# A seventh block of gate columns by seven products, q and k normalized by token tile, and the filling of the forgetting heads laid out anew

## The chip, the cores and the metric

One core of a Trainium2 chip runs the whole layer in one launch. The metric is the device time in microseconds (us). The engines named below are TensorE (PE, whose weight loads the profile lists apart as PEld), VectorE (DVE), ScalarE (ACT), GpSimd (POOL) and SyncE (SP), whose queue issues nearly all transfers.

## The reference

The layer works on x with 1024 tokens of 1024 features in float32. Half a SwiGLU network is added, then two attentions that read the same normalized tokens h, then another half network, and a gated input embedding. What the change touches is the middle:

```python
h = rms_norm(x, mix_norm)
fq, fk, fv, f_logit, sq, sk, sv, g_fox, g_sb = split_columns(h @ w_in)
fq = rms_norm(fq.reshape(b, s, 8, 64), q_norm)      # each token, each head of 64
fk = rms_norm(fk.reshape(b, s, 8, 64), k_norm)
y_fox = forgetting_attention(fq, fk, fv, log_f)     # 8 heads, softmax
y_sb = stick_breaking_attention(sq, sk, sv)         # 8 heads
merged = sigmoid(g_fox) * (y_fox @ w_branch_fox) + sigmoid(g_sb) * (y_sb @ w_branch_sb)
x = x + merged @ w_out
```

The gates g_fox and g_sb are 2048 columns of h @ w_in. The kernel counts them as sixteen gate tiles of 128 columns: 0 to 7 belong to g_fox, 8 to 15 to g_sb. They are needed only when the branches are merged, long after the heads.

## The kernel before

A float32 product is made of three passes over operands split into a high and a low part (fp32r): high by high, high by low, low by high. A product of 128 columns of w_in with 512 tokens over 1024 features takes 3 x 8 = 24 matmuls of 128x512; a gate tile has two halves of 512 tokens, so 48.

The big products are done with a scheme of seven instead of eight block products, called "seven products" here: `make_up` takes a block of 256 columns (two gate tiles) and both halves of tokens and needs seven products of 12 matmuls each (line 556), 84 instead of 96. It costs sums of weight blocks on POOL (`sums`, `last_sum`), splits on ACT and DVE, and some additions when results leave PSUM. `NG` (line 1186) is the number of blocks of 256 gate columns that go this way. Before, it is 6: gate tiles 0 to 11, from 660 to 778 us of the execution. The first block is made in the plain way (line 506), while the block products of the tokens are still being prepared; the others by seven products. The list `hl` names the SBUF slots that hold the split weights of each product, and its last names are those of the last block. `raws["v"]` and `raws["qk"]` are the weights of the next stage, loaded and split in the last products of the gates.

Then come `attention()` and its sixteen heads, eight forgetting ones (numbers 0 to 7 in the order of work) and eight of stick-breaking. A head has four steps c = 0 to 3 of 256 query tokens. `scores` makes the logits (lines 1054, 1055), and for a forgetting head subtracts and reduces on DVE (1059), takes exp on ACT (1065), a reciprocal on DVE (1066) and a product on POOL (1067). `apply`, two steps later, turns the weights with TensorE transposes (1113), splits them on ACT (1115) and DVE (1121), and multiplies with v (1139). Between these pieces of a head the program calls `take()`, which puts other TensorE work there, the filling. `fill[h]` lists the units of head h, and `take()` deals them out in shares per step. The order of TensorE's instructions is the order of these calls. That of the other engines is made by a scheduler at build time; each engine then works in order.

The filling consists of these units:

- `fox_qk_units` (line 852): the q and k columns of a pair of forgetting heads, eight units of 24 matmuls of 128x256 (line 799), one for each tile of 128 tokens. After each unit ACT squares the result (863) and copies it to N (864), and DVE sums the squares per head (865). After every fourth unit come a tensor_scalar on DVE (868), a power of -0.5 on POOL on 128x16 (869), and a product on POOL over all four token tiles, 128x1024 (871).
- `fox_stack_units` (`f[i]`, for head i + 1): four transposes (897) of the normalized q and k of 512 tokens, followed by ACT 884, DVE 885 and four transfers (887) that lay out the operands of `scores`. After each the unit yields a pause of 1.5, which counts as cost with no work.
- `v_units`: the v columns of four heads, eight units of 24 matmuls of 128x256.
- `g_units`: one gate tile, two units of 24 matmuls of 128x512 (line 807), with its own weight load and split (ACT 129, POOL 139). Tiles 12 and 13 lie in forgetting heads and are stored without sigmoid (`raw=True`); the sigmoid is then taken in `load_gate` where the branches are merged. Tiles 14 and 15 lie in stick-breaking heads.
- `sst`: operands of a stick-breaking head, two units of 24 matmuls of 128x512 (line 807 too).

PSUM banks for the filling (tag pf) and for the transposes (tag pt) are two each; a matmul that needs a bank waits until the reader of the work before last has finished.

Of the kernel before, what the change touches and what calls it, by code (L numbers as in the profile page):

```python
# [14 lines left out]
ALU = mybir.AluOpType  # L15
# [21 lines left out]
def tile_hybrid_decoder_layer(  # L37
# [811 lines left out]
    def fox_qk_units(pair, cell, tags=NAT, sq_tag="PT", new_bank=fill_bank):  # L849
        add_load(cell, lambda: mix_nat([(FQ + pair * P, FQ + pair * P + P), (FK + pair * P, FK + pair * P + P)], tags))  # L850

        def unit(t):
# [13 lines left out]
            if q == 3:  # L866
                ss = cell["ss"][half][:].rearrange("p a b -> p (a b)")
                nc.vector.tensor_scalar(ss, ss, 1.0 / HD, EPS, ALU.mult, ALU.add)
                nc.gpsimd.tensor_tensor(ss, ss, mhalf[:], ALU.pow)
                nv = N[:].rearrange("p a h s d -> p (a h s) d")  # L870
                nc.gpsimd.tensor_mul(nv, nv, ss.unsqueeze(2).broadcast_to([P, 16, HD]))
# [47 lines left out]
    def g_units(m, new_bank=fill_bank, raw=False):  # L919
        cell = {}  # L920
        if raw:
            raw_gates.append(m)

        add_load(cell, lambda: wload([kp(win)[:, :, GFOX + m * P:GFOX + m * P + P]], KD, P))

        def unit(half):
            ps = new_bank()
            yield from feat_steps(ps, half, weights(cell))
            g = slot("PT", [P, 512])
            order("act", nc.scalar.copy(g[:], ps[:]) if raw else nc.scalar.activation(g[:], ps[:], AF.Sigmoid))  # L930
            nc.sync.dma_start(gd[m, :, half * 512:half * 512 + 512], g[:])
        return [(24 * 0.216, unit(0)), (24 * 0.216, unit(1))]
# [253 lines left out]
    NG = 6  # L1186

    def mix_start():
# [18 lines left out]
        hl += [cycle[k % 6] for k in range(12, 7 * NG - 6)] + ["WL", "WH", "WH", "Q"]  # L1207
# [56 lines left out]
    def attention():  # L1264
# [8 lines left out]
        def sst(h):  # L1273
            return sb_stack_units(h - 8, stacks[h])
# [16 lines left out]
        def any_bank():  # L1291
# [11 lines left out]
        uq2, g12 = fox_qk_units(fox_pairs[2], qk[2]), g_units(12, raw=True)  # L1303
        uq3, vy = fox_qk_units(fox_pairs[3], qk[3]), v_units(SV, 0, vs0)
        g13, s8, s9 = g_units(13, raw=True), sst(8), sst(9)
# [5 lines left out]
        fill = [mix(f[0], qk1[:7]),  # L1311
                qk1[7:] + vx[:1] + f[1][:1] + vx[1:4] + f[1][1:],
                mix(f[2], vx[4:] + uq2[:3]),
                uq2[3:] + g12[:1] + f[3][:1] + g12[1:] + f[3][1:],
                mix(f[4], uq3[:6]),
                uq3[6:] + vy[:1] + f[5][:1] + vy[1:4] + f[5][1:],
                mix(f[6], vy[4:] + g13[:1]),
                g13[1:] + s8,
# [362 lines left out]
```

## Time and profile before

| what | value |
|---|---|
| median of 3 runs | 2263.2 us (2263.04 to 2263.4) |
| the profiled execution's own time | 2264.1 us |
| its span, first to last instruction | 2262.4 us |
| PE busy | 2235.7 us, 99% of the span |
| DVE, ACT, POOL busy | 1486.8, 989.3, 801.2 us |
| granted TensorE clock | 0.999 |
| forgetting heads, from the first score of head 0 to the first of head 8 | 851.3 to 1113.4 us |

In rows of the profile, "L807 PE MATMUL ps<-H,WH 128*128 128x512 f32 x384 | 115.1, 406 | 0.0" means: line 807 of the program, engine and operation, what is written from what, the shape, how many; then busy us and the mean ns of one; then idle us of the engine before them and what ended it. In a row of a window, each engine's busy us stand with the number of its instructions. A matmul's mean contains its way through a pipelined array, so matmuls follow each other faster than the mean says.

### The profile page before, as it was taken

The numbers are of one execution on the slowest core, as the hardware profiler recorded it, in microseconds if no ns is written. First come the engines' busy times: TensorE is split into PE (matmuls) and PEld (weight loads), VectorE is DVE, ScalarE is ACT, GpSimd is POOL, SyncE is SP. The second block draws the span as 40 slices with busy tenths as digits, with TensorE's granted clock in tenths as the row PEclk, the third lists the DMA queues.
The fourth block names the chain that finished last, engine by engine and source line by source line (L and its number), as shares of the span: only waits on it lengthen the run. The fifth ranks groups of instructions, "written<-read, shape, count | busy, mean of one in ns | idle before, by whom it ended". The sixth has DMA issues, their size and how long they took to land. (4 is left out here: it accounts for less than half of the span.)

```text
span 2262.4 us, 30810 instructions
## 1 busy us (share of the span) xinstructions
PE 2235.7 (99%) x11402; PEld 1900.8 (84%) x11402; DVE 1486.8 (66%) x2303; ACT 989.3 (44%) x1788; POOL 801.2 (35%) x803
## 2 busy tenths in 40 slices
PE   8999999999999999999999999999999999999999
PEld 6888888888888899999898888888888888888888
DVE  8845555688888325666678875889655555778753
ACT  6333333333364445555566663345333333433431
POOL 2444444300011336565567664410544444200121
PEclk9999999999999999999999999999999999999999
DMA  4232323484233333233323366821423232756132
GB/s 140 102 117 85 125 84 125 145 311 172 84 131 113 127 109 110 85 113 85 85 66 91 106 196 232 283 106 55 140 89 121 84 126 84 268 191 217 59 102 85
DMA packets 188936, 291.23 MB, mean 129 GB/s; under 512 B 28393, under 2 KB 104553, under 8 KB 188786
## 3 DMA queue, kind: packets, MB, share of 16 engines
q1 hardware_dynamic: 188784, 289.26, 38.5%
q8 instruction: 90, 1.47, 0.3%
q14 instruction: 60, 0.49, 0.1%
q10 hardware_dynamic: 2, 0.00, 0.0%
HBM read 193.50 MB, written 78.94 MB: 120 GB/s over the span
## 5 line engine op out<-in xcount | busy, mean ns | idle before, releaser
L454 PE MATMUL ps<-H,H 128*128 128x512 f32 x2184 | 497.7, 389 | 1.2 <-DVE X L462 1.2
L454 PEld LDWEIGHTS ps<-H,H 128*128 128x128 f32 x2184 | 409.4, 188 | 86.6 <-issue 2.0
L556 PE MATMUL ps<-H,WL 128*128 128x512 f32 x1116 | 264.9, 389 | 0.8 <-ACT WL L105 0.8
L556 PEld LDWEIGHTS ps<-H,WL 128*128 128x128 f32 x1116 | 209.4, 188 | 44.6 <-ACT WL L105 1.2
L556 PE MATMUL ps<-H,Q 128*128 128x512 f32 x612 | 146.0, 389 | 0.0
L462 DVE SCALAR_TENSOR_TENSOR X<-ps,X 128x512 f32<-128x512 f32 x168 | 109.1, 687 | 50.9 <-PE ps L454 50.9
L556 PEld LDWEIGHTS ps<-H,Q 128*128 128x128 f32 x612 | 114.9, 188 | 23.8
L556 PE MATMUL ps<-X,WL 128*128 128x512 f32 x552 | 132.6, 389 | 0.0
L139 POOL TENSOR_TENSOR WL<-RAW,WH 128x512 fp32r<-128x512 f32 (+1 forms) x84 | 98.5, 1194 | 69.1 <-ACT WH L129 43.2
L556 PEld LDWEIGHTS ps<-X,WL 128*128 128x128 f32 x552 | 103.6, 188 | 21.5
L1121 DVE TENSOR_TENSOR PT<-ps,PT 128x512 fp32r<-128x512 f32 (+1 forms) x160 | 100.0, 627 | 30.9 <-ACT PT L1115 29.7
L799 PE MATMUL ps<-WH,H 128*128 128x256 f32 x768 | 116.1, 288 | 0.8 <-ACT RN L864 0.8
L807 PE MATMUL ps<-H,WH 128*128 128x512 f32 x384 | 115.1, 406 | 0.0
L219 POOL TENSOR_SCALAR ss<-ss 128x1 f32<-128x1 f32 x28 | 9.0, 323 | 296.1 <-ACT WL L215 231.9
L1139 PE MATMUL ps<-PT,X 128*128 128x256 f32 (+1 forms) x640 | 102.7, 286 | 6.9 <-DVE PT L1121 5.8
L556 PE MATMUL ps<-H,PT 128*128 128x512 f32 x456 | 108.9, 389 | 0.0
L1115 ACT CAST PT<-ps 128x512 fp32r<-128x512 f32 (+1 forms) x160 | 87.1, 548 | 42.2 <-PE ps L1113 40.7
L1139 PEld LDWEIGHTS ps<-PT,X 128*128 128x128 f32 x640 | 90.3, 190 | 17.6 <-DVE PT L1121 10.8
L799 PEld LDWEIGHTS ps<-WH,H 128*128 128x128 f32 x768 | 101.4, 190 | 2.7 <-ACT RN L864 1.2
L556 PEld LDWEIGHTS ps<-H,PT 128*128 128x128 f32 x456 | 85.5, 188 | 17.8
L355 POOL TENSOR_TENSOR PT<-GF,RN 128x512 f32<-128x512 f32 x20 | 33.6, 1682 | 184.9 <-DVE GF L710 184.9
L1067 POOL TENSOR_TENSOR T<-T,l 128x128 f32<-128x128 f32 (+3 forms) x64 | 73.2, 1148 | 72.1 <-DVE l L1066 70.0
(436 smaller groups left out, 4889.0 us busy)
## 6 DMA issues: line engine op xcount, KB each, us to landing
hidden<-PT SPq DMA_DIRECT2D x40, 512.0 KB, 3.0
WH<-in_ffn_w_gate_dram SPq DMA_DIRECT2D x38, 512.0 KB, 5.5
Q<-hidden SPq DMA_DIRECT2D x24, 512.0 KB, 5.5
hidden<-RN SPq DMA_DIRECT2D x22, 512.0 KB, 2.6
KH<-in_ffn_w_up_dram SPq DMA_DIRECT2D x20, 512.0 KB, 6.2
KL<-in_ffn_w_up_dram SPq DMA_DIRECT2D x20, 512.0 KB, 6.8
T<-in_ffn_w_down_dram SPq DMA_DIRECT2D x20, 512.0 KB, 7.5
X<-in_x_dram SPq DMA_DIRECT2D x16, 512.0 KB, 10.2
```

Of the source, the lines that this page charges most:

```text
L139: ins = eng_lo.tensor_sub(lo[part], raw[part], f(hi[part]))
L219: nc.gpsimd.tensor_scalar(ss[:], ss[:], EPS, None, ALU.add)
L355: eng.tensor_add(s12[:, 0, :], g1[:, 1, :], g2[:, 1, :])
L454: pe(nc.tensor.matmul(groups[g][t][:], act[:, a, k, t * P:(t + 1) * P], wt[:, b, k, :], start=(fresh and n == 0), stop=(i in (6, 1, 4) and ...
L462: nc.vector.scalar_tensor_tensor(xs, groups[g][t][:], scale, xs, ALU.mult, ALU.add)
L556: pe(nc.tensor.matmul(ps[:], hl[:, a, k, :], rhs(m, b, k), start=(first and i == 0), stop=(final and i == 11), skip_group_check=True))
L799: pe(nc.tensor.matmul(ps[:, :n], hT[t // 4](a, k)[:, (t % 4) * P:(t % 4 + 1) * P], w[k // 4][b][:, k % 4, :n], start=(i == 0), stop=(i == ...
L807: pe(nc.tensor.matmul(ps[:], w[a][:, k, :], hT[half](b, k), start=(i == 0), stop=(i == 23)))
L1067: nc.gpsimd.tensor_mul(T[:, :n], T[:, :n], l[:].broadcast_to([P, n]))
L1115: high = nc.scalar.copy(pt[:, 0, :width], ps[:, :width])
L1121: ins = nc.vector.tensor_sub(pt[:, 1, :width], ps[:, :width], f(pt[:, 0, :width]))
L1139: pe(nc.tensor.matmul(o, lh, r, start=(kpair == c and i == 0), stop=(kpair == 0 and i == 3)))
```

## The change

There are three edits.

1. `NG` is 7: gate tiles 12 and 13 become a seventh block of `make_up`, ahead of the heads, and leave the filling of forgetting heads 3, 6 and 7. With them go their weight loads and splits, and their sigmoids are taken at once. The slots named for the last two products of the last block are KH and KL instead of WH twice.
2. In `fox_qk_units` the tensor_scalar, the power and the product follow every token tile, on 128x4, 128x4 and 128x256, instead of every fourth on 128x16, 128x16 and 128x1024.
3. The lists `fill[0]` to `fill[7]` are written anew. Without the gate tiles, the q, k and v units are dealt so that heads 0 to 3 have 6, 6, 6, 6 units and heads 4 to 7 have 5, 5, 5 and 1, the last with `s8` besides. The second half of the operands of head 4 (`f[3][1:]`) is now made in head 4 itself, after the first half of head 5's (`f[4][:1]`) and one q and k unit.

```diff
-            if q == 3:
-                ss = cell["ss"][half][:].rearrange("p a b -> p (a b)")
-                nc.vector.tensor_scalar(ss, ss, 1.0 / HD, EPS, ALU.mult, ALU.add)
-                nc.gpsimd.tensor_tensor(ss, ss, mhalf[:], ALU.pow)
-                nv = N[:].rearrange("p a h s d -> p (a h s) d")
-                nc.gpsimd.tensor_mul(nv, nv, ss.unsqueeze(2).broadcast_to([P, 16, HD]))
+            ss = cell["ss"][half][:, q, :]
+            nc.vector.tensor_scalar(ss, ss, 1.0 / HD, EPS, ALU.mult, ALU.add)
+            nc.gpsimd.tensor_tensor(ss, ss, mhalf[:, 0:4], ALU.pow)
+            nv = N[:, q].rearrange("p h s d -> p (h s) d")
+            nc.gpsimd.tensor_mul(nv, nv, ss.unsqueeze(2).broadcast_to([P, 4, HD]))
...
-    NG = 6
+    NG = 7
...
-        hl += [cycle[k % 6] for k in range(12, 7 * NG - 6)] + ["WL", "WH", "WH", "Q"]
+        hl += [cycle[k % 6] for k in range(12, 7 * NG - 6)] + ["WL", "KH", "KL", "Q"]
...
-        uq2, g12 = fox_qk_units(fox_pairs[2], qk[2]), g_units(12, raw=True)
-        uq3, vy = fox_qk_units(fox_pairs[3], qk[3]), v_units(SV, 0, vs0)
-        g13, s8, s9 = g_units(13, raw=True), sst(8), sst(9)
+        uq2, uq3 = (fox_qk_units(fox_pairs[i], qk[i]) for i in (2, 3))
+        vy, s8, s9 = v_units(SV, 0, vs0), sst(8), sst(9)
...
-        fill = [mix(f[0], qk1[:7]),
-                qk1[7:] + vx[:1] + f[1][:1] + vx[1:4] + f[1][1:],
-                mix(f[2], vx[4:] + uq2[:3]),
-                uq2[3:] + g12[:1] + f[3][:1] + g12[1:] + f[3][1:],
-                mix(f[4], uq3[:6]),
-                uq3[6:] + vy[:1] + f[5][:1] + vy[1:4] + f[5][1:],
-                mix(f[6], vy[4:] + g13[:1]),
-                g13[1:] + s8,
+        fill = [mix(f[0], qk1[:6]),
+                qk1[6:] + vx[:1] + f[1][:1] + vx[1:3] + f[1][1:] + vx[3:4],
+                mix(f[2], vx[4:] + uq2[:2]),
+                uq2[2:6] + f[3][:1] + uq2[6:],
+                f[4][:1] + uq3[:1] + f[3][1:] + uq3[1:3] + f[4][1:] + uq3[3:5],
+                uq3[5:] + vy[:1] + f[5][:1] + vy[1:2] + f[5][1:],
+                mix(f[6], vy[2:7]),
+                vy[7:] + s8,
```

## The prediction

> **What bounds the kernel now.** I read the page first: the engines' busy shares, then the granted clock, to see whether TensorE has anything to give.
>
> ```profile
> span 2262.4 us, 30810 instructions
> PE 2235.7 (99%) x11402; PEld 1900.8 (84%) x11402; DVE 1486.8 (66%) x2303; ACT 989.3 (44%) x1788; POOL 801.2 (35%) x803
> PEclk9999999999999999999999999999999999999999
> ```
>
> TensorE is busy for all but 26.7 us, at full clock. So a change is worth the matmuls it removes, less the idle time that it makes. Next I read the busy time by windows: first the gates, the stretch after them, and the merging of the branches; then the eight forgetting heads, one row each; then stick-breaking heads 8 to 14.
>
> ```profile
> 680.00:778.00 98.00, 98.00 (x433) 80.87 (x432) 58.61 (x96) 46.04 (x84) 17.36 (x13) 1.00 0.35 119
> 778.90:851.30 72.40, 72.40 (x519) 67.64 (x518) 19.20 (x60) 28.56 (x55) 28.41 (x23) 1.00 0.40 124
> 1400.00:1440.00 40.00, 40.00 (x178) 33.15 (x177) 25.44 (x31) 8.49 (x12) 28.82 (x24) 1.00 0.74 253
> 851.30:881.00 29.70, 28.59 (x223) 27.28 (x222) 15.19 (x60) 15.14 (x37) 18.08 (x16) 1.00 0.43 127
> 881.00:911.30 30.30, 29.11 (x230) 28.01 (x229) 19.36 (x65) 17.15 (x39) 20.32 (x21) 1.00 0.24 62
> 911.30:946.20 34.90, 34.30 (x277) 33.59 (x277) 22.85 (x73) 20.98 (x48) 19.34 (x22) 1.00 0.46 129
> 946.20:985.90 39.70, 39.52 (x278) 36.71 (x277) 21.42 (x69) 21.83 (x49) 26.42 (x25) 1.00 0.21 61
> 985.90:1018.30 32.40, 31.21 (x253) 30.63 (x253) 22.17 (x71) 18.57 (x45) 17.64 (x18) 1.00 0.42 123
> 1018.30:1051.00 32.70, 31.75 (x254) 30.80 (x253) 20.38 (x69) 19.61 (x44) 24.74 (x26) 1.00 0.28 65
> 1051.00:1083.60 32.60, 31.45 (x229) 29.45 (x230) 21.72 (x70) 18.62 (x40) 17.58 (x21) 1.00 0.41 114
> 1083.60:1113.40 29.80, 29.80 (x175) 25.82 (x174) 17.53 (x61) 16.43 (x35) 13.87 (x17) 1.00 0.22 54
> 1113.40:1334.40 221.00, 216.11 (x1326) 190.62 (x1326) 174.13 (x292) 141.66 (x314) 140.20 (x214) 1.00 0.41 111
> ```
>
> The columns are the window, its length, then busy us (instructions) of PE, PEld, DVE, ACT and POOL, the granted clock, and the DMA share with GB/s. The gates leave TensorE no idle time. The heads leave, as length less PE busy, 1.11, 1.19, 0.60, 0.18, 1.19, 0.95, 1.15 and 0.00 us: 6.37 in 262.1. Last the waits in that stretch, to see what makes them.
>
> ```profile
> PE ps L1113 <- DVE PT L1121: 3.0, 4, 1.2
> PE ps L1139 <- DVE PT L1121: 1.1, 4, 0.3
> PE ps L799 <- ACT RN L864: 0.8, 1, 0.8
> PE ps L1139 <- ACT PT L1115: 0.6, 2, 0.5
> ```
>
> In total, times, and the longest: the idle time is mostly TensorE waiting for DVE's low part (1121), which frees a transpose bank or completes an operand.
>
> **The change part by part.** *The matmuls.* In the gates 433 matmuls of 128x512 take 98.00 us, 226.3 ns each. The seventh block adds 7 x 12 = 84 of them, 19.0 us, in a stage without idle time. Two gate tiles less in the heads are 2 x 48 = 96 of the same shape, 21.7 us at the same rate. Balance -2.7 us. In the heads such a matmul also reads longer:
>
> ```profile
> L807 PE MATMUL ps<-H,WH 128*128 128x512 f32 x96 | 27.8, 404 | 0.0
> L807 PE MATMUL ps<-H,WL 128*128 128x512 f32 x48 | 13.2, 397 | 0.0
> L556 PE MATMUL ps<-H,WL 128*128 128x512 f32 x108 | 25.6, 389 | 0.0
> ```
>
> The mean of the first two is 401.7 ns against 389 in the gates, 12.7 more; 96 times that is 1.2 us. If it belonged wholly to these matmuls the balance would be -3.9. But the surplus comes from breaks between filling and head, which are as many as before and now fall on q, k and v units. I take a third, 0.4: -3.1 us.
>
> *What goes along with the gates.* A block in the gates needs POOL, ACT and DVE beside 19 us of TensorE; they have 81, 52 and 39 us free in that 98 us window, so nothing. The first matmul after the gates needs weights that are split in their last products, in slots freed a few products later than before (the low part's last slot by the seventh product of the last block, which has three products, 8.1 us, behind it). POOL does such a low part in halves:
>
> ```profile
> L139 POOL TENSOR_TENSOR WL<-PT,T x4: 1314/1318/1324, 768.4 to 772.3; 128x528 fp32r<-128x528 f32 x4
> ```
>
> Two halves are 2.6 us and fit. If that cover were gone, TensorE would wait those 2.6 us once; the window from 778.90 shows none now. On SP's queue two loads of equal bytes move there and four stores become two, at a DMA share of 0.35. The two late sigmoids leave a stage where ACT is busy 8.49 of 40 us: no gain.
>
> *Normalizing by token tile.* These are the operations in the heads (columns: busy us, mean ns, idle before), and a power and a product of nearly the new size:
>
> ```profile
> L868 DVE TENSOR_SCALAR qkss<-qkss 128x16 f32<-128x16 f32 x6 | 3.4, 566 | 0.1
> L869 POOL TENSOR_TENSOR qkss<-qkss,mhalf 128x16 f32<-128x16 f32 x6 | 17.5, 2912 | 3.0 <-DVE qkss L868 2.9
> L871 POOL TENSOR_TENSOR RN<-RN,qkss 128x1024 f32<-128x1024 f32 x6 | 11.4, 1905 | 0.5
> L220 POOL TENSOR_TENSOR rs<-ss,mhalf x32: 542/567/1612, 5.9 to 2166.7; 128x1 f32<-128x1 f32 x32
> L1067 POOL TENSOR_TENSOR T<-T,l 128x256 f32<-128x256 f32 x8 | 4.9, 614 | 4.0 <-PE ps L1113 2.0 <-DVE l L1066 1.9
> L139 POOL TENSOR_TENSOR WL<-RAW,WH 128x512 fp32r<-128x512 f32 x26 | 33.0, 1294 | 14.4 <-ACT WH L129 10.3 <-ACT PT L1115 4.2
> ```
>
> A power costs 567 ns for one column and 2912 for sixteen, 156 per column more, so about 1036 for four; a product of 256 costs 614. A token tile takes POOL 1.65 us, four of them 6.6 where 4.82 stood. Six such halves lie in the heads: +10.7 us; the splits of two gate tiles leave, four times 1294 ns, -5.2. POOL goes from 158 us busy (the sum of the eight rows) of 262 to 163 of some 240: not the bound. Its longest piece in front of a softmax product (1067) or a mask (1046) falls from 4.8 to 1.65 us. On the path to TensorE it is hidden: the transposes of q and k (897) waited for POOL nowhere above, and stand two units or more behind the last tile of their half, except `f[3][1:]`, which has one unit, 24 matmuls, and the first pieces of head 4 in front of it.
>
> *DVE's tensor_scalar* comes 24 times instead of 6 in the heads, and its rows are uneven:
>
> ```profile
> L868 DVE TENSOR_SCALAR qkss<-qkss x8: 159/182/1260, 815.1 to 1028.6; 128x16 f32<-128x16 f32 x8
> ...
> 969.62 0.41 DVE L865 TENSOR_REDUCE qkss<-PT 128x4 f32<-128x256 f32 x1
> ...
> 970.21 1.26 DVE L868 TENSOR_SCALAR qkss<-qkss 128x16 f32<-128x16 f32 x1
> ...
> 967.64 5.05 POOL L139 TENSOR_TENSOR WL<-RAW,WH 128x512 fp32r<-128x512 f32 x4 [1.93 <-ACT WH L129]
> ```
>
> At 970.21 it took 1.26 us, seven times its median, while POOL worked through four splits; the sum just ahead of it (865) kept its 0.41. Behind it on DVE wait reciprocals and line 1121, and behind that TensorE. At the mean of 566 ns, 18 more are 10.2 us of DVE; at the minimum, 2.9. DVE goes from 160.6 us of 262 to about 171 of 240, 71%. The Trainium skill, page "SBUF — State Buffer", section "Who interferes with whom", states the rule that speaks against this edit: VectorE and GpSimd share one pair of ports, a tensor_scalar in a 2-port mode can need it, and whoever comes second is blocked for the other's whole instruction. The trace agrees with 1.26 us; by that rule each of the 24 would wait for whatever POOL instruction is running, while without it they would cost about 182 ns. If what is held reaches TensorE, the sum by the rule is that of the second rival below; otherwise it stands.
>
> *The idle time with less filling.* The heads lose 22.1 us of filling (96 matmuls). Heads 0, 1, 4, 5 and 6, with little besides q, k and v units, idle 1.12 us in the mean; heads 2 and 3, with the most filling, 0.60 and 0.18; head 7, filled with 128x512 matmuls alone, 0.00. After the change heads 0 to 6 hold five or six units each, and 7 stays nearly as it is: 7 x 1.12 = 7.8 against 6.4, +1.5 us. From below, heads 8 to 14 idle 4.89 us in seven, 0.70 each, at a DVE share of 79%: eight of these are 5.6, -0.8. From above, eight of the longest, 1.19, are 9.5: +3.1. I take +1.5, since five of eight rows carry it and the extra work on DVE is paid in it.
>
> *Sum.* -2.7 - 0.4 + 1.5 = -1.6 us against the profiled execution's 2264.1: 2262.5. That execution is 0.9 above the median of the runs, 2263.2; the forecast for a median is 2261.6. A measurement of this kernel tells about 0.2%, 4.5 us, from no change, so this counts as the same.
>
> **The rivals.** *The finer pieces clear the waits* (0.25). No piece of 4.8 us stands in POOL's queue and the filling is even, so that all eight heads idle like 2, 3 and 7 now, 0.26 each: 2.1 instead of 6.4. Then -3.1 - 4.3 = -7.4: 2255.8. It counts as faster once the idle time falls by 1.4. Against it: those three heads are the ones with the most or the longest filling.
>
> *DVE is held by POOL* (0.10). The 18 added tensor_scalars are held as the six were, and every held us arrives at TensorE through line 1121: +10.2 - 3.1 = +7.1: 2270.3. It decides for slower when 7.6 of the 10.2 arrive. For it: both long rows of waits end with 1121. Against it: length less busy leaves DVE 10 us or more in every head to catch up in, and at 79% DVE heads 8 to 14 cost TensorE less.
>
> *The heads do not shrink* (0.03): their length is set by their own chains, and the gates' 19.0 come on top: 2282. Against it: head 3 has the filling of head 1 and a gate tile besides, 48 matmuls or 10.9 us, and is 9.4 us longer.
>
> **How the numbers follow.** Likeliest (0.62): 2261.6, its own range from 2263.2 - 3.9 - 0.8 = 2258.5 to 2263.2 - 2.7 + 3.1 = 2263.6. Faster has the first rival's 0.25; slower has the next two's 0.13. The range reaches down to the first rival's time, 2255.5, and up to where most of the second's 10.2 us arrive, 2268.
>
> **What would show it.** Right: windows at TensorE's full length through the gates, now some 19 us longer; 32 powers at about 1.04 us; heads together near 241 us with 6 to 9 idle; heads 8 to 14 as before. The second rival would show as tensor_scalars near 1 us with waits for 1121 behind them; the first as under 4 us idle. The forecast is wrong if TensorE waits at 778 us plus 19, for the low weights, or at line 897 in head 4.

## The result and the profile after

| | before | after |
|---|---|---|
| median of 19 runs, us | 2263.17 (2262.72 to 2263.82) | 2267.87 (2266.26 to 2269.90) |
| after to before, 95% interval | | 1.002 (1.0013 to 1.0027) |
| profiled execution, its span | 2264.1, 2262.4 | 2268.15, 2266.4 |
| first score of head 0, of head 8 | 851.3, 1113.4 | 870.1, 1117.4 |

The change makes the kernel 4.7 us slower, about 0.2%, where 1.6 us faster was forecast. The page after differs little in its totals: TensorE has 12 matmuls less, as it should (84 more, 96 less), and DVE and POOL a little more.

```profile
span 2266.4 us, 30901 instructions
PE 2235.0 (99%) x11390; PEld 1900.8 (84%) x11390; DVE 1497.9 (66%) x2337; ACT 991.0 (44%) x1793; POOL 814.8 (36%) x851
```

The windows of after tell where the time went (columns as in the prediction: the window, its length, busy us of PE, PEld, DVE, ACT, POOL, granted clock, DMA). First the gates, the stretch behind them, then heads 0 to 7, where the last row ends 1.4 us short of head 8.

```profile
660.00:797.00 137.00, 137.00 (x613) 113.32 (x612) 82.83 (x132) 68.06 (x125) 22.64 (x17) 1.00 0.34 113
797.00:870.10 73.10, 73.10 (x522) 68.20 (x522) 20.64 (x66) 29.15 (x56) 32.12 (x36) 1.00 0.39 122
870.20:896.70 26.50, 25.52 (x198) 24.40 (x197) 15.94 (x63) 14.58 (x35) 20.72 (x24) 1.00 0.48 143
896.70:928.20 31.50, 31.38 (x256) 30.81 (x255) 20.44 (x69) 18.18 (x41) 21.03 (x26) 1.00 0.26 64
928.20:961.20 33.00, 31.57 (x255) 30.68 (x254) 21.98 (x72) 20.36 (x45) 18.53 (x21) 1.00 0.43 126
961.20:993.10 31.90, 31.15 (x250) 30.33 (x249) 22.16 (x74) 18.49 (x45) 22.81 (x30) 1.00 0.14 41
993.10:1030.10 37.00, 31.58 (x234) 29.82 (x233) 22.88 (x75) 19.60 (x47) 26.71 (x32) 0.95 0.41 115
1030.10:1059.20 29.10, 28.69 (x230) 27.84 (x229) 20.33 (x69) 17.86 (x41) 22.88 (x27) 1.00 0.24 54
1059.20:1089.90 30.70, 29.17 (x229) 27.97 (x230) 21.97 (x71) 18.42 (x42) 14.30 (x19) 1.00 0.36 105
1089.90:1116.00 26.10, 25.81 (x168) 23.14 (x167) 17.19 (x61) 16.12 (x34) 15.46 (x18) 1.00 0.26 61
```

The gates have no idle time, and head 0 begins 18.8 us later, the forecast's 19.0. Seven of the heads idle about as they did. The row of 993.10 is the one to read: head 4 takes 37.0 us with TensorE busy for 31.58, 5.4 idle, and at a clock of 0.95. Its neighbour, head 5, has four matmuls less and takes 29.1. From the trace I also summed, for each head, the time from the start of each matmul to the next beyond what its shape takes in an unbroken row (227 ns for 512 columns, 120 for 256, 109 for 128). This "lost" time is used in all that follows. Before it is 2.0 to 3.4 us in heads 0 to 6 and 1.7 in head 7; after it is 1.8 to 3.8 everywhere but in head 4, where it is 9.4. Heads 8 to 14 and all that follows are as before, within 1 us.

What happens at the start of head 4 is seen in the timeline (columns: start, us of the group, engine, line, operation, out<-in, count, and the idle time ahead with what ended it). SPq is the queue of transfers.

```profile
995.24 5.48 POOL L139 TENSOR_TENSOR WL<-RAW,WH 128x512 fp32r<-128x512 f32 x4
1000.68 1.00 POOL L868 TENSOR_TENSOR qkss<-qkss,mhalf 128x4 f32<-128x4 f32 x1
1001.76 0.61 POOL L870 TENSOR_TENSOR RN<-RN,qkss 128x256 f32<-128x256 f32 x1
...
998.24 0.38 SPq L119 DMA_DIRECT2D RAW<-in_w_in_dram  x1
998.72 0.47 SPq L886 DMA_DIRECT2D Q<-KH  x1
999.28 0.54 SPq L1178 DMA_DIRECT2D y_pairs<-PT  x1
...
1004.91 0.38 ACT L863 ACTIVATE PT<-ps 128x256 f32<-128x256 f32 x1 [5.85 <-PE ps L1054]
...
997.76 0.63 PE L1112 MATMUL ps<-identf,T 128*128 128x128 f32 x4 [1.08 <-DVE PT L1120]
1002.43 0.33 PE L896 MATMUL ps<-identf,RN 128*128 128x128 f32 x1 [0.98 <-POOL RN L870]
1005.61 0.73 PE L799 MATMUL ps<-WH,H 128*128 128x256 f32 x4 [0.80 <-ACT RN L864]
1008.37 1.11 PE L1112 MATMUL ps<-identf,T 128*128 128x128 f32 x4 [2.02 <-DVE PT L1120]
```

Four things meet there. POOL makes four splits of weights in one go (995.24), and the normalizing of the last token tile of head 4's q and k stands behind them; TensorE's last transpose waits for it (1002.43). A load of weights stands at the head of SP's queue until POOL frees its RAW slot (998.24), and behind it stand the store of the head pair just finished, whose data were ready at 995.9, and the transfers of the operands. ScalarE wants to write its next square into the slot being stored, and stands still for 5.85 us (1004.91; the row names a matmul, but that was done long before; where the order is otherwise alike, as in a run below, the profile names the store). TensorE runs out of work twice more (1005.61, 1008.37). The granted clock is 0.5 for the 3.4 us after the last of these waits, worth some 1.7 us.

Before, a like group of four splits stood at 967.64 (quoted in the prediction), in the middle of head 3, with gate tile 12 for TensorE to work on; the loads behind it and the store of the pair are these rows of before:

```profile
970.22 2.87 SPq L119 DMA_DIRECT2D RAW<-in_w_in_dram  x2
...
988.22 0.58 SPq L1179 DMA_DIRECT2D y_pairs<-PT  x1
```

### The profile page after: what moved, and what is told of

Its sections match the earlier page's. It is cut to its first block, busy times and chain, and to the rows that moved or that the text cites. A ratio compares the mean times of both kernels' runs of the same rounds, so it can differ in the third digit from the quotient of the medians.

```text
span 2266.4 us, 30901 instructions
## 1 busy us (share of the span) xinstructions
PE 2235.0 (99%) x11390; PEld 1900.8 (84%) x11390; DVE 1497.9 (66%) x2337; ACT 991.0 (44%) x1793; POOL 814.8 (36%) x851
## 4 chain that ended last, share of the span: by engine, by line
PE 91%; DVE 5%; ACT 2%; issue 1%; POOL 1%; DMA 0%; DVEq 0%; ACTq 0%; POOLq 0%
PE ps L556 40%; PE ps L454 21%; PE ps L799 7%; PE ps L1596 4%; PE ps L807 4%; PE ps L1399 4%; PE ps L1138 3%; PE ps L506 2%; PE ps L1112 2%; PE ps L1054 1%; PE ps L1053 1%; PE ps L959 1%; DVE PT L1120 1%; PE ps L228 1%; DVE RN L1016 1%
## 5 line engine op out<-in xcount | busy, mean ns | idle before, releaser
L556 PE MATMUL ps<-H,Q 128*128 128x512 f32 x636 | 151.8, 389 | 0.0
L556 PE MATMUL ps<-X,WL 128*128 128x512 f32 x588 | 141.2, 389 | 0.0
L556 PEld LDWEIGHTS ps<-X,WL 128*128 128x128 f32 x588 | 110.4, 188 | 22.9
L799 PE MATMUL ps<-WH,H 128*128 128x256 f32 x768 | 121.1, 290 | 2.4 <-ACT RN L864 2.0
L139 POOL TENSOR_TENSOR WL<-RAW,WH 128x512 fp32r<-128x512 f32 (+1 forms) x80 | 92.8, 1182 | 60.0 <-ACT WH L129 39.8
L807 PE MATMUL ps<-H,WH 128*128 128x512 f32 x320 | 97.0, 407 | 0.0
L1112 PE MATMUL ps<-identf,T 128*128 128x128 f32 x576 | 89.8, 274 | 6.8 <-DVE PT L1120 6.8
```

The lines of the kernel that those rows point to most:

```text
L139: ins = eng_lo.tensor_sub(lo[part], raw[part], f(hi[part]))
L556: pe(nc.tensor.matmul(ps[:], hl[:, a, k, :], rhs(m, b, k), start=(first and i == 0), stop=(final and i == 11), skip_group_check=True))
L799: pe(nc.tensor.matmul(ps[:, :n], hT[t // 4](a, k)[:, (t % 4) * P:(t % 4 + 1) * P], w[k // 4][b][:, k % 4, :n], start=(i == 0), stop=(i == ...
L807: pe(nc.tensor.matmul(ps[:], w[a][:, k, :], hT[half](b, k), start=(i == 0), stop=(i == 23)))
L1112: pe(nc.tensor.transpose(ps[:, col:col + P], step["pr"][j][:, kb * P:(kb + 1) * P], identf[:]))
```

## The experiments

"Before" was run beside each on the same chip; the ratio is to those runs. The columns on heads are from the one profiled execution of each kernel: length of heads 0 to 7 together, then length and lost us of heads 3 and 4. That execution can lie apart from the median: by 1.3 us above it in e1 and 1.1 in e13, by 1.6 below it in e3 and e6 and 1.3 in e16. In e6 and e16 it shows no stretch of low clock in the heads, so a part of their smaller loss may be that.

| run | median us | ratio (95%) | heads 0-7 | head 3 | head 4 |
|---|---|---|---|---|---|
| before | 2263.17 | 1 | 262.1 | 39.7 / 2.0 | 32.4 / 2.6 |
| after | 2267.87 | 1.0020 (1.0013-1.0027) | 247.3 | 31.9 / 2.5 | 37.0 / 9.4 |
| e1 square in its own slot | 2268.07 | 1.0021 (1.0011-1.0030) | 248.0 | 31.2 / 1.9 | 38.2 / 10.7 |
| e2 store on ScalarE's queue | 2271.91 | 1.0035 (1.0023-1.0046) | 246.7 | 31.9 / 2.5 | 35.2 / 7.8 |
| e3 normalizing by half | 2269.10 | 1.0022 (1.0012-1.0031) | 246.0 | 31.6 / 2.2 | 35.9 / 8.5 |
| e4 before, normalizing by tile | 2263.83 | 1.0001 (0.9992-1.0010) | 262.0 | 39.7 / 2.0 | 32.4 / 2.6 |
| e5 low parts on DVE | 2266.43 | 1.0013 (1.0003-1.0022) | 245.6 | 31.9 / 2.5 | 35.3 / 7.9 |
| e6 e1 and e5 together | 2267.80 | 1.0018 (1.0008-1.0027) | 245.7 | 32.5 / 3.1 | 33.8 / 6.4 |
| e7 second half in head 3 | 2271.80 | 1.0037 (1.0024-1.0050) | 250.5 | 39.4 / 12.5 | 30.6 / 3.6 |
| e8 e7 and e5 together | 2268.47 | 1.0022 (1.0013-1.0032) | 247.7 | 36.4 / 9.5 | 30.7 / 3.7 |
| e9 gate tile 12 a second time | 2276.95 | 1.0060 (1.0046-1.0074) | 256.6 | 46.5 / 6.3 | 31.8 / 4.3 |
| e10 block of tiles 13 and 14 | 2277.74 | 1.0064 (1.0052-1.0077) | 253.0 | 39.8 / 2.1 | 30.5 / 3.7 |
| e11 transposes a unit later | 2273.79 | 1.0046 (1.0031-1.0061) | 253.3 | 31.9 / 2.5 | 41.7 / 14.3 |
| e12 pause of one unit | 2267.34 | 1.0017 (1.0007-1.0026) | 246.4 | 29.9 / 3.4 | 36.4 / 8.9 |
| e13 pause of two units | 2267.13 | 1.0017 (1.0008-1.0027) | 247.3 | 31.6 / 5.1 | 35.7 / 8.2 |
| e14 later prefetch | 2269.59 | 1.0025 (1.0015-1.0035) | 247.1 | 31.9 / 2.5 | 36.8 / 9.3 |
| e15 e14 and e12 together | 2268.17 | 1.0019 (1.0010-1.0029) | 247.0 | 29.9 / 3.4 | 37.1 / 9.6 |
| e16 next weights held back | 2265.89 | 1.0008 (0.9999-1.0017) | 243.3 | 31.9 / 2.5 | 33.5 / 6.1 |
| e17 e16 and e12 together | 2262.99 | 0.9996 (0.9988-1.0005) | 241.8 | 29.2 / 2.7 | 32.8 / 5.4 |
| e18 e17, scalars on GpSimd | 2261.11 | 0.9989 (0.9980-0.9998) | 240.7 | 29.1 / 2.6 | 32.8 / 5.4 |

### The normalizing, and single links of the chain

*e1*: the square gets a slot that is not shared with the store (smaller side buffers make room for it).

```diff
-        "Q": 2, "KH": 2, "KL": 2, "Y": 2, "PT": 4}
+        "Q": 2, "KH": 2, "KL": 2, "Y": 2, "PT": 4, "SQ": 1}
...
-    def fox_qk_units(pair, cell, tags=NAT, sq_tag="PT", new_bank=fill_bank):
+    def fox_qk_units(pair, cell, tags=NAT, sq_tag="SQ", new_bank=fill_bank):
...
```

> The changed kernel, but the square of q and k (line 863) is written to a slot of its own instead of one of the four PT slots. Theory S (in head 4 ACT is held at line 863 for 5.85 us, because the PT slot it is to write is still being stored to y_pairs; TensorE's later waits of 0.8 and 2.0 us and the 3.4 us at half clock follow from it): the hold goes, head 4 idles 2 us or less, full clock, some 4.9 us less: 2262 to 2264. Theory P (the finer pieces themselves load POOL and DVE): no change, 2267 to 2268.

Measured: 2268.07, no gain. ScalarE's hold of 5.85 us was gone, and head 4 lost more than after the change, 10.7: TensorE now waited for the transposes' low parts and for the transfers themselves. So the hold of ScalarE is not by itself what the time was lost to.

*e2*: the store of the pair is issued on ScalarE's queue.

```diff
-                nc.sync.dma_start(yd[Y["idx"], 0][:, cs], f(hi[:]))
-                nc.sync.dma_start(yd[Y["idx"], 1][:, cs], Y["t"][:, cs])
+                nc.scalar.dma_start(yd[Y["idx"], 0][:, cs], f(hi[:]))
+                nc.scalar.dma_start(yd[Y["idx"], 1][:, cs], Y["t"][:, cs])
```

> The changed kernel, but the two stores to y_pairs are issued by ACT instead of SP. If the store is late because SP's queue stands behind a weight load that waits for its slot (issue at 998.97, 3.0 us after its data), it is issued near 996.5 and lands some 2.5 us earlier: 2264 to 2266. If the landing itself is what is slow (5.5 us after the issue), it hardly moves: 2266.5 to 2268. Theory P: 2267 to 2268.

Measured: 2271.91, above all three expectations. The store went out early, at 997.35; head 4 still lost 7.8, and heads 2 and 8 lost more than before (4.2 and 6.4). Every store of every pair had moved, which may be why; it was not taken apart. The low clock came twice in this run.

*e3*: after the change, with the normalizing again after every fourth token tile. *e4*: the kernel before, with the normalizing after every tile and nothing else of the change.

```diff
 e3: in the kernel after               (e4: the same lines the other way round, in the kernel before)
-            ss = cell["ss"][half][:, q, :]
-            nc.vector.tensor_scalar(ss, ss, 1.0 / HD, EPS, ALU.mult, ALU.add)
-            nc.gpsimd.tensor_tensor(ss, ss, mhalf[:, 0:4], ALU.pow)
...
+            if q == 3:
+                ss = cell["ss"][half][:].rearrange("p a b -> p (a b)")
+                nc.vector.tensor_scalar(ss, ss, 1.0 / HD, EPS, ALU.mult, ALU.add)
+                nc.gpsimd.tensor_tensor(ss, ss, mhalf[:], ALU.pow)
...
```

> The changed kernel with edit 2 undone: power and product after every fourth token tile, edits 1 and 3 kept. Theory P: the lost time comes back, 2261 to 2264. Theory S: no gain from it, and the last transpose of head 4's operands waits for a power and a product of 4.8 us behind four splits instead of 1.65: 3 us more, 2268 to 2272.

> The kernel before with edit 2 alone: normalizing by token tile, gates and filling as they were. Theory P: slower by 2 to 7 us, 2265 to 2270. Theory S: within 1 us of before, 2262 to 2264, since no stack waits for POOL there.

Measured: 2269.10 and 2263.83, both as theory S has it. e4 is the kernel before, 1.0001, head by head. So the edit by itself costs nothing and gives nothing. In e3 head 4 lost 8.5, the largest part in one wait of 3.26 us of the transposes for POOL's product. So it isn't the cause of the loss after the change, and undoing it is no cure.

*e5*: the low parts of the fourth pair's weights are made on DVE instead of POOL. *e6*: e5 and e1 together.

```diff
...
-        uq2, uq3 = (fox_qk_units(fox_pairs[i], qk[i]) for i in (2, 3))
+        uq2 = fox_qk_units(fox_pairs[2], qk[2])
+        uq3 = fox_qk_units(fox_pairs[3], qk[3], eng_lo=nc.vector)
```

> The changed kernel, but the four low parts of the weights of the last q and k pair (POOL 139, 5.5 us in one piece at 995, between the last unit of one pair and its normalizing) are made by DVE, which is idle for 5 us then. Theory C (the second half of head 4's operands is made in head 4 by a chain with no room: q and k unit, normalizing behind four splits on POOL, transposes, transfers behind weight loads on SP that wait for the same splits, scores): POOL's piece gone, the transpose does not wait for POOL, the loads and stores of SP go out 3 us earlier; head 4 loses 4 us instead of 9.4: 2261 to 2264. Theory R (one link relieved, the wait moves to the next, as with the slot for the square): 2265.5 to 2268.

> Both together: the four low parts on DVE and the square in a slot of its own. Theory C: as the run before it or up to 2 us better, 2260 to 2263.5. Theory R: the transfers of head 4's second half still arrive after its third step asks for them, 2264 to 2268.

Measured: 2266.43 and 2267.80, both as theory R has it. Head 4 lost 7.9 and 6.4, with the waits at other places: in e5 one of 3.20 us for DVE's low part of a transpose, since DVE itself now stood behind splits. One thing in e5's trace was to be of use later. Only two of the four splits at 995 had left POOL: the other two are not the fourth pair's at all.

### Where the second half of head 4's operands is made

*e7*: the second half `f[3][1:]` goes back to the end of head 3. *e8*: e7 with e5.

```diff
-                mix(f[2], vx[4:] + uq2[:2]),
-                uq2[2:6] + f[3][:1] + uq2[6:],
-                f[4][:1] + uq3[:1] + f[3][1:] + uq3[1:3] + f[4][1:] + uq3[3:5],
+                mix(f[2], vx[4:] + uq2[:3]),
+                uq2[3:7] + f[3][:1] + uq2[7:] + f[3][1:],
+                mix(f[4], uq3[:5]),
```

> The changed kernel with the second half of head 4's operands back in head 3, right behind the last q and k unit: fill 2 has three units of the pair, fill 3 the other five and both halves, fill 4 alternates as before. Theory C: no wait for transfers or for line 863 in head 4, which loses 2 to 4 us; the last transpose of head 3 waits for its normalizing, 2 to 5 us, once. 2261 to 2265. If the place of that half is not the matter: head 4 still loses over 7, 2267 to 2270.

> The same with the four low parts on DVE: the normalizing no longer stands behind them, so the wait at the end of head 3 falls to 3 us or less. Theory C: the best of the four, 2260 to 2263. If POOL's splits were not in the way: as the run before it.

Measured: 2271.80, above both expectations, and 2268.47, above theory C but less than the run before it. Head 4 is mended (lost 3.6 and 3.7), as theory C has it, but the loss stands in head 3, larger, in a single wait. Timeline of e7:

```profile
994.55 2.47 POOL L139 TENSOR_TENSOR WL<-RAW,WH 128x512 fp32r<-128x512 f32 x2
997.00 1.88 POOL L1066 TENSOR_TENSOR T<-T,l 128x1024 f32<-128x1024 f32 x1
998.85 1.01 POOL L868 TENSOR_TENSOR qkss<-qkss,mhalf 128x4 f32<-128x4 f32 x1
999.93 0.61 POOL L870 TENSOR_TENSOR RN<-RN,qkss 128x256 f32<-128x256 f32 x1
...
1000.60 0.47 PE L896 MATMUL ps<-identf,RN 128*128 128x128 f32 x1 [9.88 <-POOL RN L870]
```

TensorE waits 9.88 us for the normalized last tile, which POOL reaches only after splits and a softmax product. Before, the 10.9 us of gate tile 12 stood between that last unit and these transposes, so that a chain of this length was covered. e8, with splits moved to DVE, shortens the wait to 6.9; so a part of the 9.88 is the queue on POOL.

*e11*: in head 4 the transposes stand behind two units instead of one.

```diff
-f[4][:1] + uq3[:1] + f[3][1:] + uq3[1:3] + f[4][1:] + uq3[3:5],
+f[4][:1] + uq3[:2] + f[3][1:] + uq3[2:3] + f[4][1:] + uq3[3:5],
```

> The change with one edit: in head 4 the transposes of the second half of its operands stand behind two q and k units instead of one, 2.7 us later. Theory C: their own wait of 0.98 us goes, but splits, store and the new pair's first units still meet there: head 4 loses 8 to 9.5 us, 2266.5 to 2268. Rival P (only the place of these transposes matters): head 4 loses 2.6 like its neighbours, 2261 to 2262.

Measured: 2273.79, both theories missed. The wait at the transposes went, but now the scores of head 4 wait for what the transposes feed:

```profile
1015.73 0.61 PE L1053 MATMUL ps<-KH,Q 128*128 128x320 f32 x1 [2.31 <-DMA Q<-KL]
1017.69 0.61 PE L1053 MATMUL ps<-KH,Q 128*128 128x320 f32 x1 [1.08 <-DMA KH<-KH]
```

So the second half has nowhere to go without loss: too early it waits for POOL, too late the scores wait for it.

### A gate tile between the pairs

*e9* makes gate tile 12 once more at the end of head 3, surplus work of 48 matmuls. *e10* gives the seventh block tiles 13 and 14, leaves tile 12 in head 3 and fills heads 0 to 3 as before.

```diff
 e9
...
-                uq2[2:6] + f[3][:1] + uq2[6:],
+                uq2[2:6] + f[3][:1] + uq2[6:] + g12,
 e10
...
-        F = make_up(N, lambda n: kp(win)[:, :, GFOX + n * 256:GFOX + n * 256 + 256], NG, tags_g, AF.Sigmoid, gate_out, load_qk)
+        F = make_up(N, lambda n: kp(win)[:, :, GFOX + n * 256 + n // 6 * P:GFOX + n * 256 + n // 6 * P + 256], NG, tags_g, AF.Sigmoid, gate_out, load_qk)
...
+                uq2[3:] + g12[:1] + f[3][:1] + g12[1:] + f[3][1:],
+                mix(f[4], uq3[:5]),
...
+                vz[2:4] + s10,  vz[4:6] + s11,  vz[6:] + s12,  s13 + g15[:1],  g15[1:] + s14,  s15,
```

> Gate tile 12 is made a second time, at the end of head 3, between the q and k units of the third and of the fourth pair; the rest is as after the change, so 48 matmuls of 128x512, 10.9 us at 226.3 ns, are surplus work. Theory C (what hurts is that the fourth pair's units follow the third pair's with no other filling between: splitting of the new weights, normalizing of the last token tile, transposes and the store of the pair all fall on the start of head 4): head 3 grows by 10.9, head 4 loses 2.5 to 3.5 us in its matmul row instead of 9.4, no stretch of half clock; 2267.9 + 10.9 - 6 to - 7 = 2271.8 to 2272.8. Rival G (less filling costs idle time wherever it is, and the wait only wanders): the surplus comes on top, 2278 to 2279, with a wait of 2 us or more somewhere else.

> As many matmuls as after the change, but the seventh block holds gate tiles 13 and 14; tile 12 stays in head 3, heads 0 to 3 are filled as before the change, head 4 with its stacks and five q and k units, 5 to 7 as after it, and heads 8 to 14 have the units of before without tile 14, dealt anew. Theory C: heads 0 to 3 take 134.5 us as before, head 4 takes before's 32.4 less one unit of 2.7, heads 5 to 7 87.4 as after: 251.6 together, 4.3 more than after; heads 8 to 14 take 10.9 less, if VectorE's 25 us a head leave it, or up to 2 us more than that. 2267.9 + 4.3 - 10.9 = 2261.3, up to 2263.3. Rival G: the idle time comes back in heads 4 to 14, 2266 or more.

Measured: in e9 head 4 loses 4.3, but head 3 now 6.3, of which one wait of 2.19 us, with the low clock after it, is the gate tile's own weights (line 129). Whatever follows the third pair at once meets the same queue of splits. The time lies between the two theories, nearer to the rival. In e10 heads 0 to 3 take 134.6 us and head 4 loses 3.7: together 253.0 for heads 0 to 7, near the 251.6 expected. So with the tile where it was, the heads come within 1.4 us of that expectation. But the whole takes 2277.74, far above theory C's 2261.3 to 2263.3 and within what rival G had: the 10.9 us taken from heads 8 to 14 are not saved at all (row of e10, then of the same heads after the change):

```profile
1123.10:1346.30 223.20, 209.74 (x1279) 183.10 (x1278) 177.19 (x292) 139.05 (x311) 141.55 (x212) 0.99 0.36 98
```

```profile
1116.00:1336.00 220.00, 214.70 (x1319) 189.41 (x1318) 172.90 (x290) 140.89 (x312) 139.12 (x211) 1.00 0.40 107
```

With filling gone, TensorE's idle time there grows from 5.3 to 13.5 us, and heads 8 to 14 take 223.2 us with 48 matmuls less against 221.4 (1117.4 to 1338.8) after the change. In the waits of e10 in that window TensorE stands 12.5 us for DVE's low part (line 1120), 6.5 ahead of the transposes and 6.0 ahead of the product with v.

### Time without work

*e12* and *e13* move one unit from head 3 to head 2 and end head 3 with a pause of one or two units' cost, which deals the units earlier and adds no work.

```diff
+        rest_ = [(2 * 1.3, iter([1.3] * 2))]          # e13: 4
...
-                mix(f[2], vx[4:] + uq2[:2]),
-                uq2[2:6] + f[3][:1] + uq2[6:],
+                mix(f[2], vx[4:] + uq2[:3]),
+                uq2[3:6] + f[3][:1] + uq2[6:] + rest_,
```

> The change, with one q and k unit moved from head 3 to head 2, and a pause of one unit's cost (2.6) dealt at the end of head 3, so that the last unit of the third pair stands some 5 us earlier relative to the start of head 4; no matmul is added. Theory T (what lacks is time between the last q and k unit and the transposes of the second half in head 4; the 9.9 us wait of the run with that half in head 3 is the whole of it): head 4 loses about 6 us in its matmul row instead of 9.4, head 3 about 3.5 instead of 2.5: 2265 to 2266. Rival W (the work that meets at the start of head 4 is too much for ScalarE, VectorE and GpSimd whenever it comes): head 4 still loses 9 us and head 3 more than before: 2268 to 2270.

> As the run before with a pause of two units' cost (5.2), the last unit some 2 us earlier still. Theory T: head 4 loses 3 to 4 us, head 3 up to 6, as the gap moves from one to the other: 2264 to 2266. Rival W: head 4 loses 9, head 3 6: 2270 to 2272.

Measured: 2267.34 and 2267.13; head 4 still loses 8.9 and 8.2. Both times lie between the two expectations, and the losses of head 4 are those of rival W: the theory that only time is lacking fell. In e12 POOL's splits did come earlier and in pieces, and still:

```profile
992.03 6.78 SPq L119 DMA_DIRECT2D RAW<-in_w_in_dram  x2
998.90 0.53 SPq L1178 DMA_DIRECT2D y_pairs<-PT  x1
...
1004.14 0.38 ACT L863 ACTIVATE PT<-ps 128x256 f32<-128x256 f32 x1 [5.02 <-DMA y_pairs<-PT]
```

Two loads of weights hold SP's queue for 6.78 us, the store stands behind them, and ScalarE behind the store.

### The prefetch

These loads are of the weights of the v units that follow, needed a head later. In the program they are asked for by the first unit of the fourth pair. *e14* asks for them at its fourth unit; *e15* adds the pause of e12.

```diff
-            weights(cell)
+            weights(cell, 1 if t < late else 2)      # late = 3 for the fourth pair
...
```

> The change with one edit: the weights of the v units that follow are fetched from the fourth q and k unit of the fourth pair on, not from its first. In the trace after the change these two loads stand on SP's queue at 998.24 and 1004.76, waiting for a RAW slot that GpSimd's splits hold, and the store of the head pair, ready at about 996, and the transfers of head 4's operands stand behind them; ScalarE then waits 5.85 us for the slot that is stored. Theory Q (this queue is the link that makes the long waits): the store goes out at about 996, ScalarE's 5.85 us wait falls under 2, and with it go TensorE's 0.80 and 2.02 us and the 3.4 us of half clock behind them; the 1.08 and 0.98 us ahead of them stay: head 4 loses 4 to 5.5 us, 2263 to 2264.5. Rival W (too much work for the engines there, whatever the queue does): head 4 loses 8 or more, 2266.5 to 2268.5.

> The run before together with the pause of one unit at the end of head 3, which brought the splits of the new weights in pieces and earlier but left the queue as it was. Theory Q: GpSimd's wait goes as well, head 4 loses 3 to 4.5, head 3 3.4: 2262 to 2264. Rival W: as after the change or worse, 2266 to 2268.

Measured: 2269.59 and 2268.17, both just above rival W, and nothing follows from it for either theory. In e14 the loads and splits stand on SP's queue and on POOL in the same order as after the change, and head 4 is the same to 0.2 us: the scheduler, it seems, moved them forward again.

*e16* holds them back with dependencies: the loads stand behind the pair's second store on SP, the splits behind the third unit's copy on ScalarE. *e17* adds the pause of e12.

```diff
+            hold["on"] = late > 0 and t == late
             weights(cell, 1 if t < late else 2)
+            hold["on"] = False
...
+            if pin is not None:
+                tc.add_manual_dep(ld.ins, pin.ins.name, NOSYNC, reason="order")
...
+        if hold["on"]:
+            tc.add_manual_dep(cp_.ins, hold["act"].ins.name, NOSYNC, reason="order")
```

> The later prefetch again, now with dependencies that keep the scheduler from moving it forward: the loads of the v units' weights stand on SP's queue behind the pair's second store, and their splits on ScalarE behind the third q and k unit's copy. Two of the four splits that GpSimd makes in one go at 995.24 after the change belong to these v units, which are not used before head 5; the other two, of the fourth pair's second half, stay. Theory Q (the prefetch, with its loads on SP's queue and its splits on GpSimd, jams the start of head 4): the store goes out at about 996.5, ScalarE's 5.85 us wait falls under 2, GpSimd's last tile is normalized 2.5 us earlier, and TensorE's waits of 0.98, 0.80 and 2.02 us go, with the half clock: head 4 loses 3.5 to 5 instead of 9.4; 2262 to 2263.8. Rival W (too much work there, whatever the order): head 4 loses 7.5 or more, 2266 to 2268.

> The run before together with a unit moved from head 3 to head 2 and a pause of one unit's cost at the end of head 3. Theory Q: nothing is left for the pause to mend; head 4 loses 3 to 5, head 3 3.4 instead of 2.5: 2262.5 to 2264.5. Rival W: 2266 to 2268.

Measured: 2265.89 and 2262.99. The heads take 4.0 and 5.5 us less than after the change. Timeline of e16 (lines 147, 1188, 873, 877, 1076, 1122 are 139, 1178, 863, 867, 1066, 1112 of after):

```profile
995.54 3.02 POOL L147 TENSOR_TENSOR WL<-RAW,WH 128x512 fp32r<-128x512 f32 x2
...
996.73 0.32 SPq L1188 DMA_DIRECT2D y_pairs<-PT  x1
...
1002.65 0.38 ACT L873 ACTIVATE PT<-ps 128x256 f32<-128x256 f32 x1 [2.14 <-PE ps L807]
...
993.68 1.89 POOL L1076 TENSOR_TENSOR T<-T,l 128x1024 f32<-128x1024 f32 x1
...
994.25 1.36 DVE L877 TENSOR_SCALAR qkss<-qkss 128x4 f32<-128x4 f32 x1
...
999.21 0.63 PE L1122 MATMUL ps<-identf,T 128*128 128x128 f32 x4 [2.67 <-DVE PT L1130]
```

Two splits instead of four, the store at 996.73 instead of 999.28, ScalarE waiting 2.14 us for its matmuls instead of 5.85, and TensorE's waits for POOL and ScalarE gone. Theory Q, the prefetch with its loads on SP and its splits on POOL, holds in its mechanism; the edit keeps back loads and splits together, so no run shows what each of the two is worth. The edit gave less than expected in e16 (head 4 loses 6.1 instead of 3.5 to 5), because a wait of 2.67 us for DVE is left. Ahead of it DVE stands 1.36 us at a tensor_scalar on 4 columns, until 995.61; POOL's product, begun at 993.68, ends at 995.57. That is the second rival of the forecast, in one place. The median, 2265.89, lies between the two expectations; that of e17 is as theory Q has it. In e17 the pause moves this tensor_scalar out of the way (0.18 us at 992.09), and the wait is 1.72.

*e18*: e17 with the tensor_scalars on GpSimd.

```diff
-            nc.vector.tensor_scalar(ss, ss, 1.0 / HD, EPS, ALU.mult, ALU.add)
+            nc.gpsimd.tensor_scalar(ss, ss, 1.0 / HD, EPS, ALU.mult, ALU.add)
```

> The run before (weights held back, pause) with the tensor_scalar of the normalizing on GpSimd instead of VectorE, at about 0.3 us each by the row of line 219 (311 ns on one column). It tells what the rival 'VectorE held by GpSimd' is worth once the jam at head 4 is cleared. If what VectorE is held for reaches TensorE (24 pieces in the heads, held ones 0.3 to 1.7 us long), the heads' loss falls by 2 us or more and the time to 2260 to 2261. If it is absorbed, as the forecast had it: within 0.7 us of the run before, 2262.3 to 2263.7; GpSimd's chain of power and product, some 0.3 us longer, would then be all that shows.

Measured: 2261.11, 0.9989 of before (0.9980 to 0.9998): faster than both kernels, by 2.2 us than before and 6.8 than after. Between the two expectations: the heads take 1.1 us less than in e17, 0.4 each in heads 0 and 1 and the rest in steps of 0.2 or less. The page's group of the moved operation and the window of the eight heads:

```profile
L877 POOL TENSOR_SCALAR qkss<-qkss 128x4 f32<-128x4 f32 x32 | 6.5, 203 | 10.4 <-DVE qkss L875 6.9 <-DVE KL L1003 1.6
```

```profile
870.40:1111.10 240.70, 233.52 (x1811) 224.74 (x1810) 155.74 (x531) 145.47 (x328) 166.99 (x215) 1.00 0.33 91
```

## Why the prediction was wrong, point by point

*The matmuls* (-2.7 and -0.4): nearly right. Head 0 begins 18.8 us later, against 19.0, and TensorE's busy time in the heads falls by 19.4 us, or 21.1 without the 1.7 that the low clock adds, against 22.1. With the jam cleared (e18, which also has a pause and the moved operation) the heads take 240.7 us, 7.2 of them idle, against the 241 with 6 to 9 idle that were to be seen.

*The gates' companions, and the late split of the next weights* (0): right. TensorE is never idle from 660 to 870 us.

*Normalizing by token tile*: the durations were right, with 1036 and 614 ns forecast and these groups of the eight heads and the stretch before them measured:

```profile
L868 POOL TENSOR_TENSOR qkss<-qkss,mhalf 128x4 f32<-128x4 f32 x32 | 32.4, 1012 | 16.8 <-DVE qkss L867 12.9 <-DVE KL L993 1.8 <-ACT KH L883 0.8
L870 POOL TENSOR_TENSOR RN<-RN,qkss 128x256 f32<-128x256 f32 x32 | 19.7, 614 | 2.5
```

e4 shows the edit to be worth nothing by itself. But the step's last sentence failed. It said that the transposes are hidden, named `f[3][1:]` as the one place with only one unit in front, and priced it at nothing. Its own wait is 0.98 us, and it is where the chain without cover shows. The prediction had named a wait at that line in head 4 (897, in after 896) as a sign that it is wrong.

*DVE held by POOL* (0 in the sum, 10.2 us as a rival): the sum was nearly right. In the heads the 24 tensor_scalars take 9.8 us, 410 ns each, where 566 were taken.

```profile
L867 DVE TENSOR_SCALAR qkss<-qkss 128x4 f32<-128x4 f32 x24 | 9.8, 410 | 0.5
```

Most of it is absorbed: taking all of them off DVE shortened the heads by 1.1 us (e18 against e17). The excess after the change is hardly from it: the two that stand beside the waits of head 4 (994.99 and 1005.78) take 0.32 and 0.17 us, and the longest of that head, 0.62, comes behind them. The Trainium skill's rule quoted in the prediction (page "SBUF — State Buffer", "Who interferes with whom") agrees with e16's row of 1.36 us beside POOL's product.

*The idle time with less filling* (+1.5): this is the step that failed. It gave every head the mean idle time of five heads of before, 1.12 us, as if filling were alike wherever it comes from and only its amount counted. Seven heads bear that out. Head 4 does not: there the order of the filling changed, with the fourth pair's units directly behind the third's. Gate tile 12 had been the cover under which weights were split, the next ones fetched, the last tile normalized and the second half laid out. e7 shows how long a wait can be without it, 9.88 us, and e10 shows head 4 near its old loss (3.7 against 2.6) with the tile in its place. The step never followed SP's queue and POOL's order across that seam, though both were in the trace of before. These are the windows of all eight heads, before and after:

```profile
851.30:1113.40 262.10, 255.73 (x1907) 242.29 (x1906) 160.62 (x537) 148.33 (x334) 158.00 (x160) 1.00 0.33 92
870.10:1117.40 247.30, 236.37 (x1811) 226.25 (x1810) 163.63 (x555) 144.95 (x328) 162.91 (x191) 0.99 0.32 89
```

In the forecast's own measure, length less busy time, the idle time goes from 6.37 to 10.93 us: +4.6 where +1.5 was forecast, and 5.42 of the 10.93 stand in head 4, which had 1.19. The low clock, for which the sum had no term, comes on top with about 1.7. So the profiled executions, 4.0 us apart where -1.6 was forecast, miss by 3.1 of idle time, 1.7 of clock and 0.8 of the matmuls. Lost time, which holds both idle time and low clock, goes from 20.7 to 27.3 us, +6.6. The medians are 4.7 us apart; single runs of after differ by up to 3.6.

*The rivals*: none of them happened. The first (finer pieces clear the waits) failed, as e4 shows; the second has the right sign and nearly the right time, 2270.3, for another reason; the heads did shrink. The measured 2267.87 lies just below 2268, the upper end that the prediction drew for most of the second rival's 10.2 us; that is luck. (The lower end, 2255.5, should have been the first rival's 2255.8.)

*What stays open*: head 4 of e18 still loses 5.4 us against 2.6 before; its largest wait, 1.72 us for DVE's low part, was not taken apart further. Whether the early loads or the early splits jam head 4 more was not taken apart. That e14 and after have one order and medians 1.7 us apart was not explained either; the kernels before beside them differ by 0.5, and the granted clock below may be part of it.

## What to carry to other kernels

Filling is not only an amount. Before a unit of it is taken away, ask what was done under it by the other engines and queues: a chain as long as the removed unit must get another cover, be moved, or be paid. When two units that feed each other's slots come to stand back to back, look at what the scheduler prefetches there: a load that is needed a head later, but stands at the head of a queue in order, holds the stores and transfers behind it. Dependencies that keep it and its splits back gave 2.0 us here by themselves (e16 against after) and 4.4 where a pause was there as well (e17 against e12). And filling taken from heads that already wait for another engine saved none of its time here (e10).

## What the runs showed of the hardware

TensorE's granted clock fell to half after a wait of 2.02 us with one of 0.80 us shortly before it. In the profiled execution after the change it is 1.00 until 1008.1; then these rows follow each other:

```profile
1004.70:1008.10 3.40, 0.85 (x5) 0.53 (x4) 2.45 (x7) 2.57 (x6) 1.63 (x2) 1.00 0.77 170
1008.10:1011.50 3.40, 3.13 (x15) 3.13 (x16) 2.58 (x10) 1.30 (x3) 0.83 (x1) 0.54 0.59 146
```

TensorE was busy for 0.85 of 3.40 us and then, from 1008.36 by the trace, ran at half speed for 3.41. In other runs a wait of 2.67 us (e16) left the clock at 1.00, and the 9.88 us of e7 brought it to half for 10.2 us. The Trainium skill, page "TensorE: Matmul & The Clock Gate", Part 1, says that activity is judged in windows of about 3.4 us that run freely; the trace agrees with that length, and with a wait of 2 us striking or not by where it falls. Counted back in steps of 3.413 us from the change of the clock at 1008.36, a window from 1004.95 to 1008.36 holds nearly the whole of both waits; counted so in e16 from its change at 2260.52, a boundary at 997.6 cuts the wait of 2.67 us, which began at 996.54, in two. The clock also orders the runs after the change: its mean is 1.0 in those of 2266.26 to 2267.22 us, 0.999 in those of 2267.73 to 2268.76 and 0.998 in those of 2269.42 and above. So the waits of 2.02 and 0.80 us cost some 1.7 us more through the clock, and not in every run.
